# Layer two's projections regrouped by norm, first transfers packed, and sums of squares, score scaling and last stores rewritten

## The chip, the cores and the metric

The kernel runs on one core of one Trainium2 chip. The metric is the device time of one execution in microseconds (us), lower is better. Every profile here is one execution recorded by the hardware profiler; its span runs from the first to the last instruction of the program.

## What is computed

A decoder trunk of two layers for 256 tokens of width 1024, all in float32, with a fixed memory of 256 rows that both layers attend to. Cut to what matters:

```
x, mem: (256, 1024)
rms(x, g) = x * rsqrt(mean(x*x, -1) + 1e-6) * g

layer one (differential attention):
  z = rms(x, a_norm_attn) @ a_w_in          # q 768 | k 768 | v 768 | memory queries 256
  q, k = rope(q), rope(k)                   # 6 heads, each with two score maps of 64
  p0, p1 = softmax(causal(q_c k_c^T / 8))   # c = 0, 1
  o = rms((p0 - lam * p1) v, subln) * 0.8   # lam from a_lambda (4 x 64)
  m = softmax(qm mk^T / 8) mv               # 4 heads; mk, mv = rms(mem, a_mem_norm) @ a_w_mem_kv
  x += [o, m] @ a_w_out
  x += relu(rms(x, a_norm_mlp) @ a_w_up)^2 @ a_w_down     # 4096 wide

layer two (with 256 tokens the block attention is plain causal attention):
  k, v = rms(x, kv_norm) @ w_kv             # 768 | 768, k with rope
  q, qm = rms(x, b_norm_attn) @ b_w_in      # 768 | 256, q with rope
  o = softmax(causal(q k^T / 8)) v          # 12 heads of 64
  m = softmax(qm mk^T / 8) mv               # mk, mv = rms(mem, b_mem_norm) @ b_w_mem_kv
  x += [o, m] @ b_w_out
  x += relu(rms(x, b_norm_mlp) @ b_w_up)^2 @ b_w_down
return rms(x, final_norm)
```

## The kernel before

**Precision.** A weight or an activation is split into a rounded part h (fp32r, the form that TensorE multiplies at full rate) and a rest l, and a product is three matmuls: h·h, h·l, l·h. ScalarE makes h (L326 for weights, L342 for activations), VectorE makes l (L328, L344).

**Weights.** `wall` holds all weights as 192 chunks of 128 x 1024 float32 (512 KB) in the order of use. A chunk lands in one of 4 buffers `w`, its h and l in one of 6 `wh` and 6 `wl`. A `w` buffer is free again when the chunk's L328 is done. All loads are issued by SyncE (SP) on one queue, in one written order.

**Activations** are kept transposed: `xT` is 128 x 8 x 256, tile k holding features 128k to 128k+127 of all tokens. A gain is applied along the partitions when a tile is split (`split_scaled`); the root of the mean square is applied later to a result, when it leaves PSUM (`evac_to`, `rope`).

**Blocks of projections** (`nat_block`, L458): four chunks are 512 columns of a weight. For each k of 8 and each half hf of the tokens, three matmuls at L473 add into one of two PSUM banks `acc` (of four). Where q and k have different norms, which is so in layer two, a block is called with two parts, `[(qT, 0, 256), (kT, 256, 512)]`, and each matmul has 256 columns. Four of layer two's blocks are made so (three blocks of q and k, and the block of the last v and the memory queries); its block of memory keys and values and its first v block have 512.

**Order of layer one** (`mixer_a`): block of q and k of pairs 4 and 5, block of pairs 0 and 1, then the memory block, the v block, and so on, with scores, softmaxes and products of earlier pairs between them.

**Roots.** `Stats.add` squares an xT tile on ScalarE (L425) and adds it up on GpSimd (POOL, L426), eight tiles; `rstd` (L429) sums over partitions with two TensorE matmuls against ones (L434), and VectorE makes the root in ten small instructions (L440, L388 to L397). Layer one's first root (`ra`) and the root for layer one's memory (`mr`) are made like this from `xT` and from the transposed memory.

**Rope** (L488): ScalarE copies a block's bank with the root as scale (L491), GpSimd multiplies by the sine (L500), VectorE by the cosine (L506) and adds (L508).

**Scores** (L512): four transposes of q and k, copies out of PSUM, matmuls into two banks (L553), the mask, then per head `mxx`: a maximum over groups of 128 columns (L564), times -0.125 (L565), a minimum of two groups (L567). ScalarE takes the exponential with scale 0.125 and that bias, and reads the sum out (L571). In `diff_T`, three small VectorE instructions (L659 to L661) make the weight of the second map.

**The last layer's end** (`mlp_last`): the down projection runs untransposed (L834), then per half of the tokens: add to x (L866), square with a sum (L868), multiply by the final gain on GpSimd (L870), the root (L874, `rsqrt_sum`), scale on VectorE (L880, columns 0 to 352 or 256) and on ScalarE (L882, the rest), and a store by SP (L884).

**The order of the work** is written by a planner (`Plan`). Each step has a cost by simple formulas, the buffers it takes and a priority: its place in the program less an offset by kind and layer (`EARLY`). Every engine takes, at each simulated moment, the ready step of lowest priority; the instructions are emitted in that order, and each engine runs its own in order. SP's loads are steps like the others, with a cost of max(450, bytes/360) ns and 1900 ns until the data counts as landed.

**The start.** x comes in four transfers of 1, 1, 2 and 4 tiles (runs of 1, 1, 2 and 4 KB for each partition), the first four chunks in halves (runs of 2 KB), the gains in one of 28 KB; the tables for rope, `subln` and `lambda` come in three small ones. The transposed memory of layer one has a buffer of its own (`B2`).

## Time and profile before

| | |
|---|---|
| time of the runs | 616.09 us median of 3, lowest 613.46 us |
| the profiled execution | 614.3 us, its span 612.5 us |
| mean granted TensorE clock | 0.994 of full speed |
| busy share | TensorE 97%, its weight loads 84%, VectorE 73%, ScalarE 63%, GpSimd 11% |
| bytes read | 104.62 MB, 173 GB/s over the span |

A busy TensorE (PE) is not a TensorE at its peak: the ends of matmuls are modelled and overlap the next ones. What counts is the distance from one start to the next, and the few places where the next start is late.

### The profile page before, as it was taken

The numbers are of one execution on the slowest core, as the hardware profiler recorded it, in microseconds if no ns is written. First come the engines' busy times: TensorE is split into PE (matmuls) and PEld (weight loads), VectorE is DVE, ScalarE is ACT, GpSimd is POOL, SyncE is SP. The second block draws the span as 40 slices with busy tenths as digits, with TensorE's granted clock in tenths as the row PEclk, the third lists the DMA queues.
The fourth block names the chain that finished last, engine by engine and source line by source line (L and its number), as shares of the span: only waits on it lengthen the run. The fifth ranks groups of instructions, "written<-read, shape, count | busy, mean of one in ns | idle before, by whom it ended". The sixth has DMA issues, their size and how long they took to land.

```text
span 612.5 us, 9943 instructions
## 1 busy us (share of the span) xinstructions
PE 597.2 (97%) x3630; PEld 516.5 (84%) x3630; DVE 449.6 (73%) x816; ACT 383.6 (63%) x780; POOL 69.7 (11%) x78
## 2 busy tenths in 40 slices
PE   7979999999999999999999999999999999999995
PEld 5867887988888888888889889989888888888884
DVE  5988899889887875655776786887997878444434
ACT  6856879767766654444665686686676665433422
POOL 1271040230000000100100201300300000000002
PEclk9989999999999999999999999999999999999998
DMA  8844365337656565655566444254466565555501
GB/s 258 292 155 140 112 198 171 117 127 219 221 180 201 178 204 174 204 174 191 186 207 215 132 138 135 74 190 155 165 214 194 184 199 181 190 189 205 187 19 68
DMA packets 30864, 106.31 MB, mean 174 GB/s; under 512 B 3680, under 2 KB 4192, under 8 KB 30816
## 3 DMA queue, kind: packets, MB, share of 16 engines
q1 hardware_dynamic: 30816, 105.69, 52.5%
q8 instruction: 28, 0.46, 0.3%
q14 instruction: 20, 0.16, 0.1%
HBM read 104.62 MB, written 1.05 MB: 173 GB/s over the span
## 4 chain that ended last, share of the span: by engine, by line
PE 94%; DVE 2%; DMA 1%; ACT 1%; issue 1%; SPq 0%; ACTq 0%; DVEq 0%
PE acc L778 29%; PE acc L473 21%; PE acc L782 15%; PE t L834 14%; PE acc L732 7%; PE t L553 2%; PE t L589 2%; PE t L646 1%; PE t L523 1%; DMA xT<-xt 1%; DVE xn L344 0%; DVE xT L718 0%; SPq L303 0%; DVE wl L328 0%; PE acc L834 0%
## 5 line engine op out<-in xcount | busy, mean ns | idle before, releaser
L328 DVE TENSOR_TENSOR wl<-w,wh 128x512 fp32r<-128x512 f32 (+1 forms) x256 | 247.8, 986 | 107.2 <-ACT wh L326 104.0
L326 ACT CAST wh<-w 128x512 fp32r<-128x512 f32 (+1 forms) x256 | 209.0, 838 | 167.7 <-PE acc L778 91.7
L778 PE MATMUL acc<-xn,wh 128*128 128x512 f32 x512 | 131.4, 396 | 0.5 <-DVE xn L344 0.5
L778 PEld LDWEIGHTS acc<-xn,wh 128*128 128x128 f32 x512 | 91.2, 188 | 18.5 <-DVE xn L344 1.8
L473 PE MATMUL acc<-wh,xn 128*128 128x512 f32 (+1 forms) x320 | 90.1, 356 | 3.2 <-ACT xn L342 2.3
L834 PE MATMUL t<-wh,B 128*128 128x512 f32 (+1 forms) x256 | 77.4, 384 | 0.0
L782 PEld LDWEIGHTS acc<-xn,wl 128*128 128x128 f32 x512 | 68.0, 188 | 5.6
L782 PE MATMUL acc<-xn,wl 128*128 128x256 f32 x512 | 69.1, 277 | 0.0
L473 PEld LDWEIGHTS acc<-wh,xn 128*128 128x128 f32 x320 | 56.0, 188 | 14.2 <-ACT xn L342 3.1
L778 PE MATMUL acc<-B,wh 128*128 128x512 f32 x256 | 64.1, 392 | 0.0
L426 POOL TENSOR_TENSOR sqa<-sqa,sq 128x256 f32<-128x256 f32 x35 | 32.6, 931 | 232.1 <-ACT sq L425 230.8
L834 PEld LDWEIGHTS t<-wh,B 128*128 128x128 f32 x256 | 47.7, 188 | 9.5
L473 PE MATMUL acc<-wl,xn 128*128 128x512 f32 (+1 forms) x160 | 55.5, 347 | 0.0
L778 PEld LDWEIGHTS acc<-B,wh 128*128 128x128 f32 x256 | 46.0, 189 | 8.2
L732 PE MATMUL acc<-B,wh 128*128 128x256 f32 x256 | 51.2, 290 | 0.0
L834 PE MATMUL t<-wl,B 128*128 128x512 f32 (+1 forms) x128 | 49.2, 384 | 0.0
L732 PEld LDWEIGHTS acc<-B,wh 128*128 128x128 f32 x256 | 41.2, 191 | 1.5 <-issue 1.2
L500 POOL TENSOR_TENSOR ropet<-ropes,trig 128x256 f32<-128x256 f32 x24 | 25.5, 1082 | 107.5 <-ACT ropes L491 93.9
L782 PEld LDWEIGHTS acc<-B,wl 128*128 128x128 f32 x256 | 34.9, 190 | 2.5
L732 PE MATMUL acc<-B,wl 128*128 128x256 f32 x128 | 36.1, 282 | 0.0
L782 PE MATMUL acc<-B,wl 128*128 128x256 f32 x256 | 35.7, 282 | 0.0
L473 PEld LDWEIGHTS acc<-wl,xn 128*128 128x128 f32 x160 | 30.1, 188 | 3.6 <-DVE wl L328 0.2
(177 smaller groups left out, 777.1 us busy)
## 6 DMA issues: line engine op xcount, KB each, us to landing
w<-wall SPq DMA_DIRECT2D x188, 512.0 KB, 3.4
w<-wall SPq DMA_DIRECT2D x8, 256.0 KB, 6.3
B<-memt SPq DMA_DIRECT2D x2, 512.0 KB, 7.8
w<-memt SPq DMA_DIRECT2D x2, 512.0 KB, 3.7
xT<-xt SPq DMA_DIRECT2D x1, 512.0 KB, 7.2
out<-qh SPq DMA_DIRECT2D x2, 256.0 KB, 2.2
out<-ql SPq DMA_DIRECT2D x2, 256.0 KB, 2.2
xT<-xt SPq DMA_DIRECT2D x2, 128.0 KB, 3.7
```

The lines of the kernel that those rows point to most:

```text
L326: P.add(("act", t_act(n), lambda sl=sl: nc.scalar.copy(h.t[:, sl], w.t[:, sl])), [(w, x) for x in q], [(h, x) for x in q])
L328: P.add(("dve", t_dve(n), lambda sl=sl: nc.vector.tensor_sub(l.t[:, sl], w.t[:, sl], h.t[:, sl].bitcast(F32))), [(w, x) for x in q] + [(h, ...
L426: P.add(("pool", t_pool(S), lambda: nc.gpsimd.tensor_tensor(self.acc.t, self.acc.t, sq.t, op=OP.add)), [sq, self.acc], [self.acc])
L473: nc.tensor.matmul(pss[hf].t[:, c0:c1], a(k)[:, ts], b.t[:, o + c0:o + c1], start=(k == 0 and i == 0), stop=(k == KT - 1 and i == 2))
L500: nc.gpsimd.tensor_tensor(t.t[:, :, o:o + 32], zs.t[:, :, 32 - o:64 - o], b(sin[:, o:o + 32]), op=OP.mult)
L523: nc.tensor.transpose(ps.t[:, i * 128:(i + 1) * 128], s(), ident)
L553: nc.tensor.matmul(sp[hd].t[:, c], qk[a].t[r, qb * 128:(qb + 1) * 128], qk[b].t[r, S:S + c.stop - c.start], start=(qb == 0 and i == 0 and ...
L589: nc.tensor.transpose(ps.t[:, i * 128:(i + 1) * 128], p.t[:, j * 128:(j + 1) * 128], ident)
L732: nc.tensor.matmul(o, a.t[:, ws], x(k), start=(n == 0 and m % 2 == 0 and i == 0), stop=(n == KT - 1 and i == 2), skip_group_check=True)
L778: nc.tensor.matmul(ps.t, wh.t[:, k * 128:(k + 1) * 128], x(k).rearrange("p a s -> p (a s)"), start=start and k == 0, stop=stop and k == 7, ...
L782: nc.tensor.matmul(ps.t[:, 0:S], wl.t[:, k * 128:(k + 1) * 128], x(k)[:, 0], start=False, stop=stop and k == 7, skip_group_check=True)
L834: nc.tensor.matmul(ps.t[:, c0:c1], a, b.t[:, c * 512 + c0:c * 512 + c1], start=(k == k0 and i == 0), stop=(k == 31 and i == 2), skip_group ...
```

## The change

1. **Layer two's blocks have one norm each.** The weights' columns are ordered anew: memory; k and v of the last third; q of the last third with the memory queries; k of pairs 0 to 3; q of pairs 0 to 3; v. Every block is `nat_block([(T, 0, 512)])`. `mixer_b` has a new order: the two half blocks, both memory scores, k block, pair 4, pair 5, q block, pairs 0 and 1, v block, pairs 2 and 3.
2. **First transfers.** Gains and x tiles 0 to 3 come as one array `xa` (4320 bytes for each partition, 553 KB), tiles 4 to 7 as `xb` (512 KB, 4 KB runs), the first chunk as two separate arrays (2 KB runs), the next three chunks whole (4 KB runs); the tables, `lambda` and `subln` are one array (`consts`, 263 KB). Order: half a chunk, `xa`, half a chunk, chunk 2, `xb`, chunks 3 and 4.
3. **Sums of squares from natural rows.** The roots `ra` and `mr` come from x and the memory in natural layout (1 MB each, two more transfers): four squares of 128 x 512 with a sum on ScalarE (`Stats.whole`), then twelve small VectorE instructions. Their sixteen squares of 256, fourteen additions on GpSimd and four of TensorE's small matmuls are gone. The transposed memory of layer one now passes through two of the four `w` buffers, as layer two's did before.
4. **Scores.** Queries leave PSUM with root/8 (`r8`), so rope's copy is two of 256 columns where a block has q and k; the maximum is two reductions with a negated result (or one of two groups), with no product or minimum after it; the exponential has no scale. `diff_T` has one small instruction in place of three.
5. **The end.** The last tile's product with the gain is VectorE's; the scale is VectorE's for the first 512 columns of a half, and split 128 / 384 for the second, whose store ScalarE issues itself.
6. **The planner** has new offsets, a start of 740 ns for loads, and a cost of max(470, bytes/290 or, above 268,800 bytes, bytes/390) ns for them.

```diff
+        idle["dma"] = 740
...
-        P.add(("dma", max(450, nbytes / 360), lambda: nc.sync.dma_start(dst(), src)), r, w, lag=1900, pri=pri)
+        P.add(("dma", max(470, nbytes / (290 if nbytes <= 2100 * 128 else 390)), lambda: nc.sync.dma_start(dst(), src)),
+              r, w, lag=1900, pri=pri)
...
+        @early("stat")
+        def whole(self, src, i):
+            t = big(i, [128, 2, D])
+            ss = fixed([128, 2, 2], "ss")
+            cells = [(c, hf) for c in range(2) for hf in range(2)]
+            dma(lambda: t.t, src, 1024 * CW, w=[(t, x) for x in cells])
+            for c, hf in cells:
+                def sq(c=c, hf=hf):
+                    v = t.t[:, hf, c * 512:(c + 1) * 512]
+                    nc.scalar.activation(v, v, AF.Square, accum_out=ss[:, c, hf:hf + 1])
...
+                nc.vector.tensor_add(ms, ss[:, 0], ss[:, 1])
+                nc.vector.tensor_scalar(ms, ms, 1.0 / D, EPS, op0=OP.mult, op1=OP.add)
+                rsqrt(self.r, ms, 2)
+                nc.vector.tensor_scalar_mul(self.r8, self.r, 0.125)
...
-            nc.vector.tensor_reduce(m, sp[hd].t[:, 0:width].rearrange("p (s n) -> p s n", s=ns), axis=AX.X, op=OP.max)
-            nc.vector.tensor_scalar_mul(m, m, -0.125)
-            if causal:
-                nc.vector.tensor_tensor(m[:, 1:2], m[:, 1:2], m[:, 2:3], op=OP.min)
+            for qb, c in enumerate((slice(0, 128), slice(128, 384))):
+                nc.vector.tensor_reduce(nm[hd][:, qb:qb + 1], sp[hd].t[:, c], axis=AX.X, op=OP.max, negate=True)
...
-            nc.vector.reciprocal(sr, rs[:, 0])
-            nc.vector.tensor_mul(sr, rs[:, 1], sr)
-            nc.vector.tensor_scalar_mul(sr, sr, nlam)
+            nc.vector.scalar_tensor_tensor(sr, rs[:, 1], nlam, ss[:, 0], op0=OP.mult, op1=OP.mult)
...
-                    P.add(("pool", t_pool(S), lambda x=x, c=c, sl=sl: nc.gpsimd.tensor_tensor(
+                    e, eng, n = ("dve", nc.vector, t_dve(S)) if last and i else ("pool", nc.gpsimd, t_pool(S))
...
-                m = 256 if c else 352
+                m = 128 if c else 512
...
+                eng = nc.scalar if c else nc.sync
...
-            pss = nat_block([(qT, 0, 512)] if qT is kT else [(qT, 0, 256), (kT, 256, 512)], ch)
+            pss = nat_block([(self.qT, 0, 512)], ch)
...
+        def half_block(self, T, z, o, evacs):
+            pss = nat_block([(T, 0, 512)])
...
+        def one_block(self, T):
+            pss = nat_block([(T, 0, 512)])
...
     def mixer_b(M, mem_kv, done):
         mem_kv()
-        M.v_block(1)
+        M.half_block(M.kT, z, 256, lambda hf: (lambda: vb[:, hf, 8:12], ("vb", 1, hf)))
+        M.half_block(M.qT, z, 0, lambda hf: (lambda: qm[hf], ("qm", hf)))
         m0 = M.mfirst(0)
-        z = M.qk_block()
+        m1 = M.mfirst(1)
+        zk = M.one_block(M.kT)
+        p4 = M.first(z, 4)
...
+        zq = M.one_block(M.qT)
...
+        p0 = M.first2(zq, zk, 0)
+        p1 = M.first2(zq, zk, 1)
+        M.v_block(0)
...
+            dma(lambda: xg[:, 0:NG + 4 * S], xa, 512 * (NG + 4 * S), w=["g"] + [("x", j) for j in range(4)], pri=-1)
+            dma(lambda: xg[:, NG + 4 * S:], xb, 512 * 4 * S, w=[("x", j) for j in range(4, 8)], pri=3)
...
+    ra.whole(xnat, 2)
+    dma(lambda: cst, consts, 512 * 513, w=["trig", "lam", "sub8"])
...
-        mr.rstd()
+        mr.whole(mnat, 3)
```

## Rows read from the trace of the kernel before

**Rows 1.** Page, part 1: busy us, share of the span, instructions of each engine.

```profile
PE 597.2 (97%) x3630; PEld 516.5 (84%) x3630; DVE 449.6 (73%) x816; ACT 383.6 (63%) x780; POOL 69.7 (11%) x78
```

**Rows 2.** Stretches: from:to, us, busy PE PEld DVE ACT POOL, clock, DMA, GB/s.

```profile
5.60:20.00 14.40, 12.30 (x48) 8.35 (x49) 11.97 (x19) 11.69 (x28) 5.83 (x7) 1.00 0.91 307
20.00:35.20 15.20, 11.85 (x55) 9.46 (x53) 14.29 (x33) 12.05 (x27) 3.68 (x6) 0.98 0.73 256
35.20:38.20 3.00, 3.00 (x7) 2.40 (x8) 3.00 (x4) 1.73 (x4) 3.00 (x3) 0.52 0.54 175
38.20:132.00 93.80, 93.80 (x611) 79.08 (x610) 80.95 (x206) 70.43 (x196) 19.02 (x20) 1.00 0.45 147
...
309.50:430.00 120.50, 120.44 (x945) 109.17 (x944) 92.39 (x197) 84.92 (x209) 14.89 (x15) 1.00 0.47 154
```

**Rows 3.** TensorE in order of time: start, us, instruction [idle before, releaser].

```profile
5.66 0.50 PE L473 MATMUL acc<-wh,xn 128*128 128x512 f32 x1 [1.17 <-ACT xn L342]
...
31.42 0.40 PE L473 MATMUL acc<-wh,xn 128*128 128x512 f32 x1
35.17 0.79 PE L473 MATMUL acc<-wh,wh 128*128 128x512 f32 x1 [3.35 <-ACT ropes L491]
```

**Rows 4.** Transfers landing data in three stretches: 0 to 3, 3 to 8, 23 to 27 us.

```profile
DMA packets 280, 0.30 MB, mean 98 GB/s; under 512 B 145, under 2 KB 152, under 8 KB 280
...
DMA packets 842, 1.27 MB, mean 254 GB/s; under 512 B 100, under 2 KB 349, under 8 KB 842
...
DMA packets 453, 1.66 MB, mean 416 GB/s; under 512 B 50, under 2 KB 50, under 8 KB 452
```

**Rows 5.** Chain that ended last, in order of time: start, us, what, instructions.

```profile
309.52 10.91 PE acc L473 x48
320.77 13.68 PE acc L473 x114
...
437.13 0.34 PE t L434 x4
...
443.17 1.86 PE acc L778 x8
445.03 0.94 PE acc L782 x8
...
518.09 85.13 PE t L834 x384
```

**Rows 6.** VectorE in order of time, the first root's last two instructions.

```profile
33.63 0.17 DVE L396 TENSOR_SCALAR rst<-rst 128x2 f32<-128x2 f32 x1
33.84 0.56 DVE L397 TENSOR_TENSOR rstd<-rstd,rst 128x2 f32<-128x2 f32 x1
```

**Rows 7.** Groups by line and form: count, busy us, mean ns of one, idle before.

```profile
L763 ACT ACTIVATE u<-u 128x512 f32<-128x512 f32 x32 | 20.2, 630 | 3.0 <-DVE u L760 3.0
...
L564 DVE TENSOR_REDUCE nm<-t 128x3 f32<-128x384 f32 x24 | 13.2, 550 | 0.7 <-PE t L553 0.6
...
L565 DVE TENSOR_SCALAR nm<-nm 128x3 f32<-128x3 f32 x24 | 4.3, 179 | 0.8
```

**Rows 8.** The same view, ScalarE alone, 330 to 400 us (layer two's attention).

```profile
L571 ACT ACTIVATE B<-t,nm 128x256 f32<-128x256 f32 x16 | 7.5, 477 | 3.1 <-DVE nm L565 3.1
L571 ACT ACTIVATION_READ_ACCUMULATOR B<-t,nm 128x1 f32 x24 | 4.9, 205 | 0.0
L621 ACT ACTIVATE B<-B,rs 128x256 f32<-128x256 f32 x9 | 4.4, 519 | 0.0
...
L530 ACT CAST qh<-t 128x512 fp32r<-128x512 f32 x6 | 3.4, 590 | 0.4 <-PE t L523 0.4
```

**Rows 9.** VectorE and SP at the end, in order of time.

```profile
606.85 0.40 DVE L403 SCALAR_TENSOR_TENSOR rst<-rstd,part 128x1 f32<-128x1 f32 x1
607.28 0.16 DVE L404 SCALAR_TENSOR_TENSOR rst<-rst 128x1 f32<-128x1 f32 x1
...
608.86 0.81 SPq L884 DMA_DIRECT2D out<-ql  x2
```

More of the change, by code (lines that the diff above doesn't have):

```diff
@@ L222, in tile_hybrid @@
 @with_exitstack
-def tile_hybrid(ctx: ExitStack, tc: tile.TileContext, xt, memt, wall, gains, fgain, subln, lam, trig, out):
+def tile_hybrid(ctx: ExitStack, tc: tile.TileContext, xa, xb, memt, xnat, mnat, w0, wall, consts, fgain, out):
     nc = tc.nc
@@ L533, in scores @@
             passes = ((0, 0), (0, 1), (1, 0))
-        ns = 3 if causal else 2
-        nm = [fixed([128, ns], "nm") for _ in range(2)]
+        nm = [fixed([128, 2], "nm") for _ in range(2)]
         ss, rs = [fixed([128, 2, 2], n) for n in ("ss", "rs")]
@@ L926, in first, with first2 @@
             return scores([lambda hf=hf, o=o: z[hf].t[:, o + c:o + c + 128] for o in (0, 256) for hf in range(2)],
-                          z, True)
+                          [(x, o) for x in z for o in ((0,) if self.diff else (0, 256))], True)
+        def first2(self, zq, zk, pr):
+            c = pr * 128
+            return scores([lambda hf=hf, z=z: z[hf].t[:, c:c + 128] for z in (zq, zk) for hf in range(2)],
+                          [(x, 0) for x in zq + zk], True)
         def mfirst(self, jm):
@@ L973, in mixer_a @@
         M.dout(o45, (4, 5))
-        p2 = M.first(z, 2)
-        p3 = M.first(z, 3)
+        p2 = first(z, 2)
+        p3 = first(z, 3)
         t2 = turn(p2)
@@ L1099, in tok, with nat_rows @@
         return a.reshape(S, KT, 128).transpose(2, 1, 0)
+    def nat_rows(a):
+        return a.reshape(2, 128, D).transpose(1, 0, 2)
     def nat(w):
```

188 lines of the change are left out of this document (99 added, 89 removed).

## The prediction

> **What bounds the kernel.** The page's busy times come first: TensorE is busy for 97% of the span, the next engine, VectorE, for 73% [rows 1]. So an edit changes the time only if it shortens TensorE's stream or a pause in it. The stretches say where the pauses are [rows 2]: from 38.2 us on TensorE is busy throughout; in 5.6 to 20 us it is busy 12.3 of 14.4, in 20 to 35.2 us 11.85 of 15.2, and in the 3 us after that its clock is 0.52, near the lower level (1.2 GHz). Block one's 48 matmuls fill the first of these stretches. TensorE's order in time shows the large pause [rows 3]: the last start of block two is at 31.42 us, the memory block's first at 35.17. Its bank of PSUM is held until rope has copied it, and that copy waits for the first root. From the chain I take the prices of matmuls [rows 5]: 10.91/48 = 0.227 us for 512 columns and 13.68/114 = 0.120 for 256, on the same line.
>
> Two blocks without a pause are 96 x 0.227 = 21.8 us. The first starts at 5.66 [rows 3], the third could at 27.5; it does at 35.17. These 7.7 us, 1.5 us of half clock (seven matmuls in 3.05 us, 35.17 to 38.22, for 1.59), and the tail after the last matmul are what can be had without taking work off TensorE.
>
> **First transfers and root of x (parts 2 and 3).** What lands by 3 us is 0.30 MB; from 3 to 8 us, where runs are of 1 and 2 KB (349 of 842 packets under 2 KB), 254 GB/s move; from 23 to 27 us, with 4 KB runs, 416 [rows 4]. First matmul: it needs 262 KB and `xa`, 815 KB; the 0.51 MB left at 3 us take 1.2 to 2.0 us more. Today's 0.42 MB would be there at 3.5 us by the same rate, and the first matmul is 2.1 us after that [rows 3], a lag in which later transfers move and tile 0 is split. So 7.1 us at worst, and 5.3 if `xa`, one piece, lags by half as much behind 4.2; I take 6.0, a little later than now. Block one: all its data is 3.17 MB, of which 2.87 come after 3 us, so it is there at 10.3 us at 416 GB/s and 14.7 at 254. Without a pause TensorE needs the last chunk's h and l, 1.4 us of splitting, at 6.0 + 36 x 0.227 = 14.2 us. I take the side of 416, since all but 0.5 MB has runs of 4 KB, and 0.5 us of small waits: block one ends at 17.4, block two at 28.3.
>
> The root: 3.17 MB, 0.26 MB of tables, at most 2.1 MB of block two's weights and the 1.05 MB of x rows, 6.6 MB, land at 18.5 us (416 GB/s) to 28.2 (254). Four squares of 0.63 [rows 7] with a read of the sum of 0.205 [rows 8] are 3.3 us. Twelve small VectorE instructions are 2 us at 0.17, and 6.7 at the 0.56 that half of them take today while GpSimd adds squares beside them [rows 6]; these additions are gone, so I take 2.2. With rope's copy (0.7) and 2 us in ScalarE's and VectorE's queues behind splits the bank is free at 27 us; bounds 25 and 41. I place the memory block at 28.8: 0.5 us of waiting after block two. The gain is 35.17 - 28.8 = 6.4, and the clock does not fall: 1.5 more. **-7.8 us**; bounds -9.5 (5.3 us and no waits) and 0 (254 GB/s throughout).
>
> Here a rule speaks against the packing: the Trainium skill, "DMA: Bandwidth & Descriptors", Specifications, has transfers at line rate from 512 bytes on, so that runs of 4 KB would win nothing over 1 KB. By it, 254 GB/s is the start's own rate; block one's last chunk would be ready at 16.1 us and the block would end at 18.8, 1.4 us later than in my sum. The rows differ from it, 254 against 416, but they also differ in place.
>
> The second root loses four small TensorE matmuls (0.34 us [rows 5]): **-0.3**. Its 1 MB transfer, its squares (as long as the eight they replace) and its VectorE work lie beside the 93.8 us from 38.2 on, in which VectorE is busy 81 and ScalarE 70 [rows 2]; uncovered they would hold the memory block's two banks, and the block after next would wait. The memory tiles now pass through the `w` ring: SP, in order, then queues weights behind them. Their splits are the same instructions as before, and TensorE has 11 us of v block before it is short. I take 0.
>
> **Layer two's blocks (part 1).** 384 matmuls of 256 columns become 192 of 512: 2 x 0.120 - 0.227 = 0.0127 us each, **-2.4**. Bounds: 0.94/8 and 1.86/8 from the MLP give 192 x 0.0025 = 0.5; 0.2217 (85.13/384) for the wide one gives 3.5 [rows 5]. A rule again: "TensorE: Matmul & The Clock Gate", Back-to-back issue gap, of the Trainium skill gives N/2.4 + 2.5 ns for an isolated matmul, so a pair of 256 costs 2.5 ns more than one of 512; that is 0.5 us in all. The row of this line says 12.7.
>
> The new order moves each block's four loads on SP's queue and its splits past score work. Rope's copies, sines and products keep their columns, in eight calls for six; about 1 us more on ScalarE and GpSimd each, where TensorE never waits in 309.5 to 430 (0.06 us idle [rows 2]). If that cover went, the block after next would lack a bank. 0, from -1 to +4, the upper end being a pause like the one at 31.42.
>
> **Scores (part 4).** One reduction of 384 at 0.55 and two instructions of 0.18 [rows 7] become two reductions, 0.28 + 0.42 by a slope of 1 ns per column (an estimate); 0.2 us less for each of 24 heads, and less in `diff_T`. Rope's split copy adds a quarter of a microsecond to ScalarE six times. All is off TensorE's path, under 81 of 93.8 us of VectorE: 0, or up to -1.5 where VectorE is last.
>
> **The end (part 5).** The product with the gain, now VectorE's, stands before the root: at most the 0.42 of an addition there. In return the root's third instruction loses what GpSimd costs it, 0.40 against 0.16 next to it [rows 9]. ScalarE scales 384 columns where it had 160 and 256; the stores go out from two queues, so that the second need not follow the first by 0.4 us (0.81 for two [rows 9]). Near 0; -0.3 to +0.4.
>
> **Sum.** 614.3 - 7.8 - 0.3 - 2.4 = **603.8 us**. The profiled execution (614.3; span 612.5) stands 0.3% under the median shown and 0.1% over the lowest run. Two per cent, about what a measurement of this kernel tells from no change, is at 603.8 from the median and at 602.0 from the profiled execution.
>
> **Rivals.**
> *A, the root stays late.* Its transfer has a low priority, and SP stands in order behind loads that wait for VectorE's splits. For it: VectorE is busy 14.3 of 15.2 us before 35.2 [rows 2]. Against: nothing in block two's loads waits for TensorE. Memory block at 33, half clock kept: 614.3 - 2.2 - 0.3 - 2.4 = 609.4 (607 to 611).
> *B, all ends good:* -9.5, -0.3, -3.5 and up to -1.5 by a lighter VectorE: 599.5 to 601.
> *C, the packing doesn't do what it says:* supply stays at 254 GB/s over the first 3 MB whatever the runs. 603.8 + 1.4 = 605.2. The first of the two pages' rules would make it so.
> *D, wide matmuls are no cheaper than two halves:* 192 x 0.0025 us: 605.7. The second page's rule says this; the chain's two prices on one line speak against it.
> *E, slower.* Place: layer two's end of attention. The four pairs 0 to 3 now all wait for the q block, where before they came after two blocks. Price: a pair costs ScalarE 2 x (0.477 + 0.37 + 2 x 0.205) for exponentials (0.37 for 128 columns by 0.83 ns a column), 1.04 for two products, 0.59 for the copy [rows 8], two more copies at most as long: 5.3, four pairs 21 us. If ScalarE, in order, starts them only after the v block's copies, the output projection's first four chunks (4 x 24 x 0.120 = 11.5 us) are the only cover: a pause of 9.8 us and half clock after it, 1.5: 615.1. It decides where pause and half clock pass 10.5 us together. Against it: ScalarE is busy 85 of 120.5 us there, and the v block covers 11 us more.
>
> **Chances.** Forecast 0.50 (601 to 606.5), A 0.15, B 0.13, C 0.08, D 0.08, E 0.04, other losses 0.02. The range 599.5 to 610 leaves out E, the others and the edges of A and B. Faster by over 2%: B and under half of the forecast, 0.36; slower: E and a little, 0.05; within: 0.59.
>
> **What would show it.** Memory block's first start near 28.8 us and clock 1.0 after it (A: a start past 32); block one ending by 18 (C: near 19); 0.227 for layer two's matmuls in rows without a 256 (D: more); TensorE busy throughout to the last matmul (E: a pause after the v block); last matmul to the span's end still 7 us. The forecast is wrong if TensorE pauses for over 3 us anywhere after 30 us.

## The result, and the profile after

| | before | after |
|---|---|---|
| median of the runs | 615.21 us (5 runs) | 608.11 us (5 runs, 607.27 to 609.46) |
| profiled execution (span) | 614.3 us (612.5) | 608.1 us (606.3) |
| ratio of the runs | | 0.990, 95% interval 0.987 to 0.993 |

The change gains 1.0% (0.7 to 1.3%). One of the five runs before took 1519.66 us and is left out of the ratio; the other four have a median of 614.5 us. The forecast was 603.8 us, range 599.5 to 610, and "within 2%" the likeliest class: range and class hold. But of the 10.5 us forecast for the profiled execution 6.2 came, and the 4.3 us that are missing are nearly all in the first 40 us.

The page of the changed kernel, part 1, answers [rows 1]: TensorE has 3.1 us less of busy time and its share is 98%; VectorE is 14 us lighter, which moved nothing.

```profile
PE 594.1 (98%) x3430; PEld 505.6 (83%) x3430; DVE 435.5 (72%) x790; ACT 380.6 (63%) x780; POOL 58.5 (10%) x67
```

Stretches of the changed kernel, with the columns of [rows 2]: the start in four pieces, then the stretch up to layer one's MLP, then layer two from its first block to its up projection.

```profile
5.30:20.00 14.70, 14.62 (x56) 11.88 (x57) 12.10 (x26) 10.91 (x23) 0.00 (x0) 1.00 0.95 339
20.00:31.00 11.00, 9.45 (x42) 7.42 (x40) 6.28 (x22) 8.22 (x22) 0.00 (x0) 1.00 0.90 329
31.00:33.95 2.95, 2.88 (x12) 2.17 (x12) 2.16 (x4) 2.95 (x11) 2.85 (x2) 1.00 0.83 250
33.95:36.70 2.75, 1.61 (x5) 0.71 (x5) 2.11 (x4) 2.75 (x9) 0.57 (x2) 1.00 0.70 285
36.70:125.50 88.80, 88.64 (x587) 74.41 (x587) 72.71 (x177) 68.60 (x195) 15.72 (x16) 1.00 0.48 161
305.60:419.80 114.20, 114.20 (x730) 95.81 (x729) 85.96 (x182) 78.20 (x196) 13.77 (x17) 1.00 0.49 162
```

TensorE is busy throughout from 36.7 us on, as before from 38.2. Layer two's attention takes 114.2 us where it took 116.7 (309.36 to 426.07): 2.5 less. What is left of pauses lies between 29 and 37 us, and there is a new one: in the fourth stretch TensorE is busy for 1.61 of 2.75 us. The DMA queues are busy for 0.95 and 0.90 of the first two stretches, at 339 and 329 GB/s, where [rows 2] has 0.91 and 0.73, at 307 and 256 (its second stretch reaches to 35.2 us).

The clock of 1.00 in the first row says nothing of its first four microseconds: the trace's records of the clock begin at 9.34 us, at the upper level. Up to there the matmuls stand 0.43 us apart, as they do where a clock of 0.51 is on record (e9 below).

TensorE in order of time, after, answers [rows 3]: start, us, instruction, [idle before, releaser].

```profile
5.38 0.79 PE L493 MATMUL acc<-wh,xn 128*128 128x512 f32 x1 [0.52 <-ACT xn L346]
6.40 1.05 PE L493 MATMUL acc<-wh,xn 128*128 128x512 f32 x2
...
29.05 0.40 PE L493 MATMUL acc<-wh,xn 128*128 128x512 f32 x1
31.07 0.50 PE L493 MATMUL acc<-wh,wh 128*128 128x512 f32 x1 [1.62 <-ACT ropes L516]
...
34.61 0.49 PE L493 MATMUL acc<-wh,wh 128*128 128x512 f32 x1 [0.51 <-ACT wh L330]
35.34 0.50 PE L493 MATMUL acc<-wl,wh 128*128 128x512 f32 x1 [0.23 <-DVE wl L332]
...
36.48 0.50 PE L493 MATMUL acc<-wh,wh 128*128 128x512 f32 x1 [0.41 <-ACT ropes L516]
```

The pause ahead of the memory block shrank from 3.75 us between starts to 2.02, and both blocks ended 2.4 us sooner; together the block starts 4.1 us sooner, at 31.07. In return three starts inside the block are late, by 0.67, 0.50 and 0.57 us beyond the usual 0.227, 1.74 together.

ScalarE of the changed kernel in order of time, around the root. The natural rows of x land at 23.2 us, four squares follow, the root (VectorE, L433 to L436) is done at 28.13; the copies that free the bank (L516) start at 30.19, behind two casts (L330), of which the second waited for its chunk. Then come the four squares of the memory's rows, from 32.11, ahead of the second copies at 35.60, although their sums are first read at 52.5 us.

```profile
23.20 0.63 ACT L428 ACTIVATE B<-B 128x512 f32<-128x512 f32 x1 [2.55 <-DMA B<-xnat]
...
25.67 2.10 ACT L346 ACTIVATE wh<-w,xT 128x256 fp32r<-128x256 f32 x5
27.83 1.14 ACT L330 CAST wh<-w 128x512 fp32r<-128x512 f32 x2
29.14 1.14 ACT L330 CAST wh<-w 128x512 fp32r<-128x512 f32 x2 [0.17 <-DMA w<-wall]
30.19 0.83 ACT L516 ACTIVATE ropes<-acc,rstd 128x256 f32<-128x256 f32 x2
...
32.11 0.63 ACT L428 ACTIVATE B<-B 128x512 f32<-128x512 f32 x1
...
35.60 0.83 ACT L516 ACTIVATE ropes<-acc,rstd 128x256 f32<-128x256 f32 x2
```

VectorE, the first root after (answers [rows 6]; first and last of twelve instructions): each takes 0.16 to 0.17, none 0.56. Behind them, in order, come splits of the transposed memory (L348).

```profile
25.79 0.16 DVE L433 TENSOR_TENSOR ms<-ss 128x2 f32<-128x2 f32 x1 [4.34 <-ACT B L428]
...
27.96 0.17 DVE L436 TENSOR_SCALAR rstd<-rstd 128x2 f32<-128x2 f32 x1
28.08 2.07 DVE L348 SCALAR_TENSOR_TENSOR wl<-w,xT,wh 128x256 fp32r<-128x256 f32 x5
```

SP's queue after: the 1 MB of rows (xnat) is issued at 15.90 us, behind loads that SP held back (4.94 us for two, 6.31 for four); 4.2 us of these waits the trace puts down to VectorE's splits of weights (L332), which free the buffers. Further on, the third chunk of the memory block is issued only at 29.78 us. SP waited 5.5 us for it, until a split of the transposed memory (L348), which now passes through two of the four `w` buffers.

```profile
3.07 4.94 SPq L307 DMA_DIRECT2D w<-wall  x2
...
9.54 6.31 SPq L307 DMA_DIRECT2D w<-wall  x4
15.90 0.42 SPq L307 DMA_DIRECT2D B<-xnat  x1
...
22.54 0.42 SPq L307 DMA_DIRECT2D B<-mnat  x1
29.78 17.93 SPq L307 DMA_DIRECT2D w<-wall  x8
```

Transfers that land data from 3 to 8 us, and from 9 to 13, after (answers [rows 4]): 391 GB/s where 254 moved, and then, while SP waits, 247.

```profile
DMA packets 602, 1.96 MB, mean 391 GB/s; under 512 B 67, under 2 KB 67, under 8 KB 602
...
DMA packets 333, 0.99 MB, mean 247 GB/s; under 512 B 35, under 2 KB 35, under 8 KB 333
```

The chain that ended last, layer two's blocks after (answers [rows 5]): 26.82/117 = 0.229 us a matmul of 512 columns, where two of 256 cost 0.240.

```profile
305.77 7.51 PE acc L493 x33
313.62 26.82 PE acc L493 x117
```

Groups of VectorE by form, after (answers [rows 7]): the maximum is 0.28 + 0.41 us for a head, where 0.55 + 0.18 + 0.18 stood.

```profile
L595 DVE TENSOR_REDUCE nm<-t 128x1 f32<-128x256 f32 x24 | 9.9, 412 | 0.0
L595 DVE TENSOR_REDUCE nm<-t 128x1 f32<-128x128 f32 x24 | 6.8, 282 | 0.4 <-PE t L580 0.3
```

The end, after (answers [rows 9]): VectorE's product with the gain, the root's third instruction, and the two stores, 0.25 us apart. From the last matmul's start (598.85) to the span's end are 7.50 us; before 7.44 (605.09 to 612.53).

```profile
600.22 0.42 DVE L898 TENSOR_TENSOR ql<-ql,ropet 128x256 f32<-128x256 f32 x1 [0.64 <-ACT sq L895]
...
600.93 0.22 DVE L399 SCALAR_TENSOR_TENSOR rst<-rstd,part 128x1 f32<-128x1 f32 x1
...
602.80 0.34 SPq L914 DMA_DIRECT2D out<-ql  x1
603.05 0.34 ACTq L914 DMA_DIRECT2D out<-ql  x1
```

### The profile page after: what moved, and what is told of

Its sections match the earlier page's. It is cut to its first block, busy times and chain, and to the rows that moved or that the text cites. A ratio compares the mean times of both kernels' runs of the same rounds, so it can differ in the third digit from the quotient of the medians.

```text
span 606.3 us, 9487 instructions
## 1 busy us (share of the span) xinstructions
PE 594.1 (98%) x3430; PEld 505.6 (83%) x3430; DVE 435.5 (72%) x790; ACT 380.6 (63%) x780; POOL 58.5 (10%) x67
## 3 DMA queue, kind: packets, MB, share of 16 engines
HBM read 106.72 MB, written 1.05 MB: 178 GB/s over the span
## 4 chain that ended last, share of the span: by engine, by line
PE 91%; DMA 3%; DVE 2%; ACT 2%; issue 0%; SPq 0%; DVEq 0%; ACTq 0%
PE acc L805 29%; PE acc L493 18%; PE acc L809 15%; PE t L861 14%; PE acc L759 7%; PE t L580 2%; DMA w<-wall 2%; PE t L618 2%; PE t L675 1%; DVE wl L332 1%; PE t L551 1%; ACT wh L330 1%; DMA w<-w 1%; DVE xT L745 0%; ACT B L599 0%; PE acc L861 0%
## 5 line engine op out<-in xcount | busy, mean ns | idle before, releaser
L332 DVE TENSOR_TENSOR wl<-w,wh 128x512 fp32r<-128x512 f32 (+1 forms) x256 | 244.7, 976 | 118.8 <-ACT wh L330 118.1
L330 ACT CAST wh<-w 128x512 fp32r<-128x512 f32 (+1 forms) x256 | 208.4, 843 | 174.5 <-PE acc L805 91.5
L805 PEld LDWEIGHTS acc<-xn,wh 128*128 128x128 f32 x512 | 91.1, 188 | 18.5 <-DVE xn L348 1.8
L493 PE MATMUL acc<-wh,xn 128*128 128x512 f32 x256 | 88.4, 407 | 0.5 <-ACT xn L346 0.5
L493 PEld LDWEIGHTS acc<-wh,xn 128*128 128x128 f32 x256 | 49.1, 192 | 12.1 <-ACT xn L346 0.8
L493 PE MATMUL acc<-wl,xn 128*128 128x512 f32 x128 | 50.8, 397 | 0.0
L759 PE MATMUL acc<-B,wh 128*128 128x256 f32 x256 | 49.9, 288 | 0.0
L446 POOL TENSOR_TENSOR sqa<-sqa,sq 128x256 f32<-128x256 f32 x21 | 20.9, 993 | 229.4 <-ACT sq L445 228.8
L527 POOL TENSOR_TENSOR ropet<-ropes,consts 128x256 f32<-128x256 f32 (+1 forms) x28 | 26.6, 970 | 119.8 <-ACT ropes L516 99.6
L599 ACT ACTIVATE B<-t,nm 128x128 f32<-128x128 f32 (+1 forms) x64 | 27.1, 455 | 3.5 <-DVE nm L591 2.4
```

Of the source, the lines that this page charges most:

```text
L330: P.add(("act", t_act(n), lambda sl=sl: nc.scalar.copy(h.t[:, sl], w.t[:, sl])), [(w, x) for x in q], [(h, x) for x in q])
L332: P.add(("dve", t_dve(n), lambda sl=sl: nc.vector.tensor_sub(l.t[:, sl], w.t[:, sl], h.t[:, sl].bitcast(F32))), [(w, x) for x in q] + [(h, ...
L446: P.add(("pool", t_pool(S), lambda: nc.gpsimd.tensor_tensor(self.acc.t, self.acc.t, sq.t, op=OP.add)), [sq, self.acc], [self.acc])
L493: nc.tensor.matmul(pss[hf].t[:, c0:c1], a(k)[:, ts], b.t[:, o + c0:o + c1], start=(k == 0 and i == 0), stop=(k == KT - 1 and i == 2))
L527: nc.gpsimd.tensor_tensor(t.t[:, 0:nh, e:e + 32], zs.t[:, 0:nh, 32 - e:64 - e], b(sin[:, e:e + 32]), op=OP.mult)
L599: nc.scalar.activation(p[hd].t[:, c], sp[hd].t[:, c], AF.Exp, bias=nm[hd][:, qb:qb + 1], accum_out=ss[:, hd, qb:qb + 1])
```

## Experiments

All kernels are the changed kernel with an edit; times stand against runs of the kernel before on the same chip (medians 614.4 to 614.8 us there). "Memory block" is its first matmul, "MLP" the first matmul of layer one's MLP, both us from the span's start. The intervals of most overlap with that of the changed kernel: the verdicts rest on places in the trace, and the times of those kernels only bound them. In e1, e2, e3, e7, e11 and e14 the planner writes the order anew with the edit; the others keep the changed kernel's order but for the steps that are named.

| kernel | time, us | ratio to before (95%) | block two's last start | memory block | MLP | span |
|---|---|---|---|---|---|---|
| before | 615.2 | | 31.42 | 35.17 | 129.29 | 612.5 |
| after | 608.1 | 0.990 (0.987 to 0.993) | 29.05 | 31.07 | 125.57 | 606.3 |
| e7_old_root | 613.5 | 0.998 (0.997 to 1.000) | 29.11 (root's last matmul) | 33.44 | 128.43 | 611.9 |
| e2_halves | 610.9 | 0.996 (0.994 to 0.997) | 27.95 | 31.72 | 126.27 | 609.1 |
| e3_short_runs | 608.1 | 0.990 (0.989 to 0.992) | 28.18 | 30.87 | 125.39 | 606.4 |
| e1_root_early | 609.3 | 0.992 (0.990 to 0.994) | 29.66 | 33.82 | 128.88 | 609.7 |
| e8_load_first | 608.6 | 0.990 (0.987 to 0.993) | 29.56 | 31.77 | 126.27 | 607.0 |
| e9_memsq_late | 608.1 | 0.989 (0.985 to 0.992) | 28.81 | 31.02 | 125.31 | 606.1 |
| e10_warm_too | 607.9 | 0.989 (0.986 to 0.992) | 29.99 | 31.93 | 126.16 | 607.0 |
| e11_old_end | 607.5 | 0.988 (0.985 to 0.991) | 28.35 | 30.24 | 124.77 | 605.4 |
| e12_copy_first | 607.6 | 0.990 (0.987 to 0.993) | 29.00 | 29.23 | 124.67 | 605.5 |
| e13_copies_first | 607.2 | 0.989 (0.987 to 0.991) | 29.58 | 29.82 | 124.38 | 605.2 |
| e14_with_old_end | 607.4 | 0.989 (0.987 to 0.991) | 29.62 | 29.84 | 125.61 | 606.2 |
| e15_memrows_late | 609.1 | 0.992 (0.990 to 0.993) | 28.81 | 29.04 | 126.13 | 606.9 |

### The parts, undone one at a time

**Root of x from the transposed tiles (e7).**

```diff
-    ra.whole(xnat, 2)
+    for k in range(KT):
+        ra.add(lambda k=k: xT[:, k], [("x", k)])
+    ra.rstd()
```

> The changed kernel, but x's first root is made from the transposed tiles again (eight squares, GpSimd additions, four small matmuls), so the 1 MB load of natural x rows is gone; the memory's root stays as changed. Theory (the old way is late because VectorE's twelve small instructions run at 0.56 us beside GpSimd's additions and stand behind splits): memory block's first start at 32 to 35 us, half clock after it, time 609 to 612. Rival (the old root's data is there at 13 us, so that without the late 1 MB transfer the root is earlier): start at 29.3 to 30.5, time 606 to 607.5.

Span 611.9, time 613.5, against 614.6 for before on that chip and 609 to 612 expected. The memory block starts at 33.44, 2.4 us later than after, and the clock is 0.63 in the mean of the stretch 28.9 to 38.1; at the MLP's start 2.9 us of the 3.7 that the start gained are gone. The other 2.7 us by which the span is longer than after's lie in later stretches that the edit doesn't touch (1.2 in layer one's MLP, 1.1 in layer two's up projection, 0.3 between), and their cause was not found. TensorE, then ScalarE, in order of time in this kernel: the copy waits for the root's last instruction (L462), as it did before.

```profile
33.44 0.80 PE L493 MATMUL acc<-wh,wh 128*128 128x512 f32 x1 [4.07 <-ACT ropes L516]
```

```profile
32.54 0.84 ACT L516 ACTIVATE ropes<-acc,rstd 128x256 f32<-128x256 f32 x2 [0.49 <-DVE rstd L462]
```

So the natural rows carry most of what the start gained, by the places in the trace, as far as one run shows in which the planner's order changed too. Block one runs in this kernel without the long pauses of before, so that those went for another reason than the squares of x.

**Layer two's blocks in halves of 256 columns (e2).** Both loops over a block get two parts again; the new order of the weights stays.

```diff
-            pss = nat_block([(T, 0, 512)])
+            pss = nat_block([(T, 0, 256), (T, 256, 512)])
```

> The changed kernel, order of the blocks kept, but layer two's four blocks with rope are each made as two parts of 256 columns with the same norm: 384 matmuls of 256 in place of 192 of 512. Theory (a pair of 256 costs 0.0127 us more than one of 512): the stretch from layer two's first block to its up projection grows by 2.4 us (114.2 to 116.6), time about 610.5. Rival (0.0025 us a pair, as the isolated spacing has it): 0.5 us, 608.6.

From layer two's first block to its up projection 116.27 us pass (306.31 to 422.58), 2.04 more than after, for 192 pairs: 10.6 ns each, near the 12.7 worked out from the chain of before. Time 2.8 us longer than after; the other 0.7 us are at the start (the memory block at 31.72), where this edit changes nothing but what the planner makes of it: a pause of 3.77 us, and a clock of 0.50 from 33 to 35 us. The chain of waits in this kernel has the narrow price again, 0.127 us in a piece that holds both widths:

```profile
314.32 27.74 PE acc L493 x219
```

**First transfers cut up again (e3).** `xa` in pieces of 1, 1 and 2 tiles, the first four chunks in halves with runs of 2 KB.

```diff
-            dma(lambda: xg[:, 0:NG + 4 * S], xa, 512 * (NG + 4 * S), w=["g"] + [("x", j) for j in range(4)], pri=-1)
+            dma(lambda: xg[:, 0:NG + S], xa[:, 0:NG + S], 512 * (NG + S), w=["g", ("x", 0)], pri=-1)
+        if k in (1, 2):
+            a, b = NG + k * S, NG + 2 * k * S
+            dma(lambda a=a, b=b: xg[:, a:b], xa[:, a:b], 512 * (b - a), w=[("x", j) for j in range(k, 2 * k)], pri=k - 0.5)
...
-            first_ch.append(chunk(2 if k == 0 else 1))
+            first_ch.append(chunk(2))
```

> The changed kernel with its first transfers cut up again: gains with x tile 0, tile 1, tiles 2 and 3, and chunks 2 to 4 in halves (runs of 1 to 2 KB), all else kept. Theory (long runs move at 350 to 420 GB/s, short ones at 254): block one is short of data, the last start of block two comes at 30 to 31 us instead of 29.05, time 1 to 1.5 us longer (609 to 609.6). Rival (run length does nothing): 29.05 within 0.3, time 608.

The time is the same, 608.13 against 608.11. Transfers landing from 3 to 6 us, then 8 to 10, in this kernel: with 254 of 471 packets under 2 KB the rate is 223 GB/s (after: 377 in the same three microseconds); with runs of 2 and 4 KB it is 390.

```profile
DMA packets 471, 0.67 MB, mean 223 GB/s; under 512 B 54, under 2 KB 254, under 8 KB 471
...
DMA packets 289, 0.78 MB, mean 390 GB/s; under 512 B 31, under 2 KB 31, under 8 KB 289
```

The packing does raise the rate, then; whether by longer runs or by fewer transfers this run does not separate. But in pieces the first tile lands at 3.84 us instead of 4.80, the first matmul starts at 4.62 instead of 5.38, and block two ends 0.9 us sooner, not later. The copies still start at 29.99 us, so that this goes into a longer pause (2.69 us) and a clock of 0.50 behind it. The packing buys no time. Nor does it explain block one's long pauses of before: they are absent here too, and what removed them is left open.

### Why the memory block starts at 31 us and not at 28.8

**The root's transfer with a high priority (e1).** `ra.whole(xnat, 2)` gets the priority 4, and the planner writes the whole order anew.

> The changed kernel with one edit: the 1 MB of natural x rows is loaded before chunk 4 instead of after chunk 8. Theory (the memory block waits for the first root, and the root for a transfer that SP holds back behind loads which wait for w buffers): the memory block's first matmul starts right behind block two, at 29.3 to 30 us instead of 31.07, and the time falls by 1 to 2 us, to 606 to 607. Rival 1 (the queues of ScalarE and VectorE set the root, not the transfer): the start stays at 31 and the time at 608. Rival 2 (1 MB ahead of chunk 4 starves block one): a pause before 29 us, time 609 or more.

The rows landed at 12.97 us and the root was done at 23.2, five microseconds sooner; the memory block came 2.7 us later (in a profiled execution of 611.4 us; the others took 609.2 to 609.3). TensorE in order of time in this kernel shows why: the planner, which now believed that the first rope would be early, had put transposes of pair 4 (L551) ahead of the block, and they waited for rope's last addition on VectorE.

```profile
29.89 0.27 PE L551 MATMUL t<-ident,B 128*128 128x128 f32 x1
32.41 1.76 PE L551 MATMUL t<-ident,B 128*128 128x128 f32 x7 [2.25 <-DVE B L535]
```

The run says nothing about the root as such: an edit of a priority changes every queue. The next ones keep the planned order and move single steps in it.

**The transfer alone, moved behind the third chunk (e8).**

```diff
+    done = P.order()
+    loads = [st for st in done if st.eng == "dma"]
+    done.remove(ra.load)
+    done.insert(done.index(loads[5]) + 1, ra.load)
```

> The changed kernel with one transfer moved: the 1 MB of x in natural rows is issued right behind the third chunk of weights; every engine's order of work stays as in the changed kernel. Theory (the root is late because its transfer waits in SP's queue behind loads that wait for weight buffers, landing at 23.2 us): it lands by 15 us, the root is done by 26 us, the memory block starts at 28.7 to 29.8 us instead of 31.07, and the time is 606 to 607 us. Rival 1 (the memory block is held by its own weights and splits, which come later by as much as the moved transfer takes on the DMA queue): it starts at 30.5 us or later, time 608 us or more. Rival 2 (block one's last chunks come later by the 2.5 us of the moved megabyte, and blocks one and two end later): block two's last start moves from 29.05 to 30 us or later, time 608 to 610 us.

The theory fell. The root was done at 27.04 us, 1.1 sooner, and the memory block started 0.7 us *later*: 0.2 of it because the pause was no shorter, 2.21 us between starts (the first rival), and 0.5 because block two ended later. That is not the second rival: no matmul of blocks one and two waits, in either kernel, but here ten intervals of 0.43 us stand at the start in place of eight. ScalarE in this kernel: the copies stand, in order, behind casts, the first of which waits 1.81 us for its chunk, which the earlier megabyte had pushed back.

```profile
28.47 1.14 ACT L330 CAST wh<-w 128x512 fp32r<-128x512 f32 x2 [1.81 <-DMA w<-wall]
29.85 1.14 ACT L330 CAST wh<-w 128x512 fp32r<-128x512 f32 x2 [0.23 <-DVE wl L332]
30.89 0.83 ACT L517 ACTIVATE ropes<-acc,rstd 128x256 f32<-128x256 f32 x2
```

**The memory's squares ten instructions later (e9, on top of e8).**

```diff
+    acts = [st for st in done if st.eng == "act"]
+    late = acts[max(acts.index(st) for st in mr.squares) + 10]
+    for st in mr.squares:
+        done.remove(st)
+    at = done.index(late) + 1
+    done[at:at] = mr.squares
```

> As the kernel with the moved transfer, and the four squares of the memory's rows stand ten instructions later in ScalarE's order. Theory (the stalls of 0.67, 0.50 and 0.58 us in the memory block of the changed kernel come from these squares standing ahead of casts and rope copies that TensorE waits for): the three stalls go, 1 to 1.7 us less than the kernel with the moved transfer alone, 604.5 to 606 us. Rival (the memory block waits for its own weights, the squares only stand beside that wait): the stalls stay or shift to later banks, and the time is within 0.4 us of the other's.

The three stalls of 0.67, 0.50 and 0.57 us are gone, as the theory has it; its time is not: 608.1 us where 604.5 to 606 were expected, 0.5 less than e8. After a pause as long as in e8 (2.21 us between starts) the clock fell to its lower level in this execution, which the same pause had not done in e8. The stretch from 32.0 to 35.5 us (columns of [rows 2]) has it: clock 0.51, ten matmuls.

```profile
32.00:35.50 3.50, 3.50 (x10) 2.71 (x10) 1.78 (x3) 2.60 (x7) 0.99 (x2) 0.51 0.75 294
```

Eight intervals of 0.43 in place of 0.227 are 1.6 us, about what the stalls had cost: memory block to MLP is 94.29 us here and 94.50 in e8. And at half speed TensorE waits less for its weights in any case, so this run does not price the squares. The next one, e10, has the same order of work and kept its clock (1.00). There the block still waits 0.13 and 0.92 us beyond the usual interval, for the cast and the split of a chunk that came late. By e10 against e8, then, about 0.7 of the 1.76 us that e8 loses there are the squares'.

```profile
34.91 0.51 PE L495 MATMUL acc<-wh,wh 128*128 128x512 f32 x1
36.06 0.50 PE L495 MATMUL acc<-wl,wh 128*128 128x512 f32 x1 [0.64 <-DVE wl L332]
```

**No idle stretch before the first matmul (e10, on top of e9):** 44 small matmuls instead of 34, which compute nothing that is used.

```diff
-    for _ in range(34):
+    for _ in range(44):
```

> As the kernel with moved transfer and late squares, and 44 instead of 34 small matmuls before the first real one, so that TensorE has no idle stretch before it; they compute nothing that is used. Theory (in the changed kernel the granted clock stands at its lower level until 9.3 us, eight matmuls of 0.43 us in place of 0.227, because TensorE was idle before the first; with an early root block one's end decides): the clock is at its upper level by 6 us, block one ends 0.5 to 1.5 us sooner, time 0.3 to 1.5 us less than without. Rival (block one is bound by what lands, not by TensorE): block one's end stays within 0.3 us and so does the time.

The rival's cause holds for this run, not its 0.3 us: with 0.227 us matmuls from the start, TensorE waits 1.05 and 0.50 us at 6.8 and 8.1 us for casts and splits of weights, and block two's last start is at 29.99, 1.2 us later than in e9. But e9 was no fair partner, since in its execution the clock had risen by itself at 4.8 us, by the first clock record of its trace. What the lower level costs at the start is read better from pairs with nearly the same order there: e8 and e9 (29.56 and 28.81), the changed kernel and e11 (29.05 and 28.35), e13 and e15 (29.58 and 28.81), the first of each at 0.43 us a matmul until 9 to 10.4 us. It is 0.7 to 0.8 us, from one execution of each.

**Rope's copies ahead of the casts (e12, on top of e9).** The two copies of the first half stand ahead of the four casts before them in ScalarE's order.

```diff
+    first, second = ([st for st in r if st.eng == "act"] for r in sorted(roped[:2], key=lambda r: r[0].start))
+    acts = of("act")
+    ahead(first, acts[acts.index(first[0]) - 4])
```

> As the kernel with moved transfer and late squares, and in ScalarE's order rope's two copies of block one's first half stand ahead of the four casts of weights that they stood behind (two of which waited for their chunk to land). Theory (the pause before the memory block is no longer the root's, which was done at 26.3 us there, but ScalarE's order: the copies started at 30.1): the copies run at 26.5 to 28 us, the memory block starts by 29.5 us within 0.6 us of block two's last start (2.2 us with the copies behind the casts), the clock stays at its upper level there, and the time falls by 1.5 to 3.5 us, to 604.5 to 606.5; the second half's copies may stop the block once after its twelfth matmul for up to 1 us. Rival (the memory block's weights, delayed by the copies or landed late, hold it in place of the copies): it starts at 30.5 us or later, or loses the same 2 us within its first 24 matmuls, time within 0.7 us of 608.

This is what the prediction had hoped for: the block starts at 29.23, 0.23 after block two's last start, with no pause and the clock at its upper level. ScalarE, then TensorE, in this kernel:

```profile
26.63 0.84 ACT L521 ACTIVATE ropes<-acc,rstd 128x256 f32<-128x256 f32 x2
28.42 1.14 ACT L330 CAST wh<-w 128x512 fp32r<-128x512 f32 x2 [0.96 <-DMA w<-wall]
```

```profile
30.23 0.50 PE L495 MATMUL acc<-wl,wh 128*128 128x512 f32 x1 [0.61 <-DVE wl L332]
...
34.14 0.49 PE L495 MATMUL acc<-wh,wh 128*128 128x512 f32 x1 [1.07 <-ACT wh L330]
34.86 0.50 PE L495 MATMUL acc<-wl,wh 128*128 128x512 f32 x1 [0.23 <-DVE wl L332]
```

Of the 1.84 us by which the block starts sooner than after, 0.9 are left at the MLP (124.67 against 125.57): the block now waits inside itself, 0.78, 1.25 and 0.51 us beyond the usual interval, for splits and casts of its weights. The time, 607.6 us, is over the 604.5 to 606.5 expected. Both theories had a part: the order on ScalarE held the start, and the rival's "loses the same within its first 24 matmuls" holds for what came behind it.

**Both halves' copies (e13), and the old end with it (e14).** e13 moves the second half's copies and the product with the cosine ahead in the same way; e14 adds the old end of e11.

```diff
+    prod = next(st for st in done if st.eng == "dve" and st in sorted(roped[:2], key=lambda r: r[0].start)[0])
+    dves = of("dve")
+    ahead([prod], dves[dves.index(prod) - 4])
+    acts = of("act")
+    ahead(second, acts[acts.index(second[0]) - 2])
```

> As the one before, and also the copies of block one's second half ahead of the two casts before them, and the product with the cosine (VectorE) that frees their buffer ahead of four splits. Theory (ScalarE's order again: the second half's bank is what the memory block waits for at its thirteenth matmul): no pause over 0.3 us from block two to the end of the memory block, time 0.3 to 1 us less than the one before, 603.5 to 606. Rival (the chunks' landings are the bound by then, each behind the last on SP's queue): the pause moves to a wait for a cast or a split, time within 0.3 us of the one before.

> As the one before with the end of the kernel before (gain on GpSimd, columns split at 352 and 256, both stores by SP). Theory (the old end was 0.2 us shorter, 7.3 against 7.5 us from last matmul to the span's end): 0.2 us less than the one before, not to be told apart by the times. Rival: 0.5 us or more either way.

e13 reaches the MLP at 124.38, 1.2 us sooner than the changed kernel, and its median is 0.9 us lower, a difference that the intervals do not settle; 603.5 to 606 were expected. Three pauses of 0.30, 0.52 and 0.51 us remain in the block, all for casts and splits: the rival's side of it. e14 has the same order up to there, and in its execution the memory block lost 1.26, 0.40 and 0.51; its median is not to be told apart from e13's.

**The memory's rows behind the block's weights (e15, on top of e13).**

```diff
+    loads = of("dma")
+    last = loads[loads.index(mr.load) + 2]
+    done.remove(mr.load)
+    done.insert(done.index(last) + 1, mr.load)
```

> As the kernel with both halves' copies ahead, and the 1 MB of the memory's natural rows is issued behind the next two chunks of weights instead of ahead of them (its squares stand late in ScalarE's order already). Theory (with the copies out of the way the memory block is bound by what lands: its second to fourth chunks come in beside this megabyte): TensorE's pauses in the memory block, 0.52 + 0.30 + 0.51 us in the kernel before this one, fall by 0.5 to 1.3 us together, time 606 to 607. Rival (the chunks wait for weight buffers that VectorE's splits free, not for the transfer): the casts wait as before and the pauses stay within 0.3 us, time 607 to 607.6.

Half of the theory holds: the two pauses of 0.52 and 0.51 us are gone, and the block's third and fourth chunks landed 3.3 us after their issue, 4.5 and 4.4 in e13. But the one of 0.30, for a split, has become 1.50, so that the weights also had 1.2 us more; that this alone does not remove them is seen in e14, which waited 1.26 us at the same place and kept 0.40 and 0.51. The time is longer, not shorter. The megabyte now delays a chunk of the v block, and its cast stands in ScalarE's order ahead of the copies that free the v block's bank. ScalarE, then TensorE, in this kernel:

```profile
39.03 1.14 ACT L330 CAST wh<-w 128x512 fp32r<-128x512 f32 x2 [3.27 <-DMA w<-wall]
40.08 0.83 ACT L521 ACTIVATE ropes<-acc,rstd 128x256 f32<-128x256 f32 x2
```

```profile
40.96 0.50 PE L495 MATMUL acc<-wh,xn 128*128 128x512 f32 x1 [1.97 <-ACT ropes L521]
```

It is the wait of 29 to 31 us once more, ten microseconds later.

### The end

**The old end (e11):** gain on GpSimd, columns split at 352 and 256, both stores by SP.

```diff
-                    e, eng, n = ("dve", nc.vector, t_dve(S)) if last and i else ("pool", nc.gpsimd, t_pool(S))
+                    e, eng, n = "pool", nc.gpsimd, t_pool(S)
...
-                m = 128 if c else 512
+                m = 256 if c else 352
...
-                eng = nc.scalar if c else nc.sync
+                eng = nc.sync
```

> The changed kernel with the end of the kernel before: product with the gain on GpSimd, columns split at 352 and 256, both stores issued by SP. Theory (the new end gains nothing: what the root's third instruction wins, 0.40 to 0.22 us, the longer scale on ScalarE and the addition on VectorE take back): last matmul to the span's end within 0.2 us of the changed kernel's 7.5, time within 0.4 us of 608. Rival (the new end wins but something else lost as much): 0.5 us longer or more.

Last matmul's start to the span's end: 598.06 to 605.36, 7.30 us, 0.2 less than after; e14 has 7.30 as well. The theory holds; the new end is worth nothing, if anything a fifth of a microsecond the wrong way. The shorter span of this execution (605.4) comes from its start, where the memory block began at 30.24.

## Why the prediction was right, and where it was not

**First transfers and root of x: -7.8 forecast, -3.8 came** (4.1 by the earlier memory block, 1.46 by the clock that did not fall, less 1.74 of stalls inside the block). Step by step:
- First matmul: 6.0 forecast, 5.38 measured. Block two's end: 28.3 forecast, 29.3 measured (29.05 and one interval). Its first matmuls stood 0.43 us apart, the spacing of the lower clock level, eight times, for which the sum had no term; by the three pairs named at e10 that is 0.7 us of the 1.0. Block one ended at 18.3 us, between the sign for the forecast (18) and C's (19).
- The root's transfer: forecast to land between 18.5 and 28.2, taken near the early end; it landed at 23.2. SP issued it at 15.90, behind loads that waited in part for buffers, which is rival A's mechanism.
- Squares (2.6 us; 3.3 forecast) and VectorE's part (2.3; 2.2 forecast) came as costed, and the 0.56 us instructions went with GpSimd's additions.
- **The step that failed is "I place the memory block at 28.8: 0.5 us of waiting after block two".** The prediction treated the root as the last thing that the copy needs. The 2 us it gave for the queues were there (28.13 to 30.19), but as casts with a wait for a chunk in them, not as a fixed delay behind the root: in e8 the root was done 1.1 us sooner and the copies ran later. With the copies ahead of the casts (e12, e13) the block starts within 0.24 us of block two's last start. So the root's landing set the time only down to a point that in-order ScalarE fixed.
- What was missing altogether is the price of the second root at this place. Its squares were costed at nothing, "beside the 93.8 us from 38.2 on"; the planner put them at 32.1 to 35.6 us, ahead of casts and copies that TensorE waits for. Of the 1.74 us of stalls there about 0.7 are theirs (e10 against e8).
- The memory's tiles in the `w` ring were taken at 0 too, since "TensorE has 11 us of v block before it is short". It ran short in the memory block: SP waited 5.5 us with the third chunk for a buffer that the transposed memory held, whose splits stood on VectorE, in order, behind a root that had waited 4.34 us for its squares. The chunk landed at 33.5 us, 2.4 us after the block's start; before, all four had landed by 32.1, 3.1 us ahead of it. No run moved this wait alone, so its price is not shown.
- Behind these stands the supply: the two natural arrays add 2.1 MB to the first 35 us, in which the queues move 329 to 339 GB/s, 6 us' worth. The prediction counted the first for the root's landing, and neither for the weights that land after them. This account is argued from the rates, not measured in all. Each experiment that freed one queue met the next chunk's landing (e8, e12, e15).
- The prediction's landing times (10.3 and 14.7, 18.5 and 28.2 us) are 0.4 us later than 3 us plus the bytes left over its rates, and nothing in it says why. The forecast does not hang on that; C's 605.2 becomes 604.8.

**Second root's small matmuls: -0.3 forecast, not seen.** From the memory block to the MLP pass 94.12 us before and 94.50 after. Taking 1.46 us of half clock off the one (3.05 less 1.59) and 1.74 of stalls off the other leaves 92.66 and 92.76.

**Layer two's blocks: -2.4 forecast, -2.5 measured** (116.71 to 114.23), and 2.04 of it comes back when the halves do (e2). By the Trainium skill, "TensorE: Matmul & The Clock Gate", Back-to-back issue gap, whose formula for isolated matmuls (N/2.4 + 2.5 ns) makes two of 256 columns 2.5 ns dearer than one of 512, it would have been 0.5 us, an estimate. The 10.6 ns a pair of e2 stand against that, as the chain of before did. No pause at layer two's end of attention, so rival E has nothing.

**Scores: 0 forecast.** VectorE lost 14 us of busy time and 0.22 us a head (0.2 forecast), and layer two gained no more than its matmuls explain. **The end: 0 forecast**, 0.06 longer, and e11 shows the pieces cancel.

**The rivals.** A named the right queue, but its place (33 us) and the half clock are those of e7, not of this kernel; what happened lies between A and the forecast. C's premise is wrong, since the supply did rise to 391 GB/s, and its conclusion, that the packing saves nothing, is right by e3 for another reason: the wait for the copies hides it. The rule behind C is line rate from 512 bytes on (the Trainium skill, "DMA: Bandwidth & Descriptors", Specifications). In this start, cutting the transfers into pieces with runs of 1 and 2 KB took the rate from 377 to 223 GB/s in the same three microseconds, which does not agree with it, though the number of transfers changed as well.

In sum 6.2 us of span: 3.7 at the MLP's start and 2.5 in layer two. The measured 608.1 lies outside the forecast's own band (601 to 606.5) and inside A's (607 to 611). That the time fell in the range is owed to bounds that took in A, and so in part to luck; the middle was 4.3 us too low.

## What to carry to other kernels

When a wait is about to be removed, list in order what stands on the queue of the engine that must act next, ahead of the instruction that is needed, and what each of these waits for: here the copies that free a bank stood behind casts that waited for weights, and an earlier root alone bought nothing. Extra bytes in a start that is already bound by supply are paid by whatever lands after them, so cost a new transfer there at its full time. And place "hidden" work by where the order really puts it, not by the stretch that has room.

## What the runs showed of the hardware

- A pause of about 2 us left the granted clock at its upper level (1.00) in some executions (after, 2.02 us between starts; e8, 2.21) and was followed by the lower one in another with the same pause (e9, 2.21: 0.51 from 32.0 to 35.5 us); pauses of 2.7 us (e3, then 0.50 from 31 to 33 us) and 4.3 (e7, 0.50 from 33 to 35) were followed by the lower level too. A pause near 2 us has no one price: 0 or 1.6 us more.
- After the same 34 small matmuls the first real ones ran at 0.43 us each until 9 to 10.4 us in some executions (after, e8, e13, e14) and at 0.227 nearly from the start in others (e9, e11, e12, e15), though TensorE's idle time before the first was about a microsecond or less in all. The clock column reads 1.00 in both cases, since it counts the time before the first clock record as full; that record begins at 9.34 us in the changed kernel, at 10.30 in e8 and at 4.76 in e9. It cost 0.7 to 0.8 us of the 1.6 to 2 that the slower matmuls themselves took; in the fast starts some matmuls waited for weights (0.5 us at 6.9 us in e9).
